# Gate and up projections of two feature blocks from seven half-width products in place of eight, in a two-layer fp32 decoder on one core

## Chip, cores and metric

The kernel runs on one core of a Trainium2 chip. The metric is the device time of one execution in microseconds (us). Before the change it was 2683.49 us, the median of 3 runs (2681.64 to 2683.74).

## What is computed

The reference is two layers of a decoder trunk on 512 tokens of width 1024. Each layer is a SwiGLU feed-forward block at half weight, a mixer (stick-breaking attention and a Mamba2 scan), and a second feed-forward block. The part that the change touches is the feed-forward block, of which there are four:

```
def swiglu(h, w_up, w_down):
    gate, up = jnp.split(h @ w_up, 2, axis=-1)
    return (jax.nn.silu(gate) * up) @ w_down
...
x = x + 0.5 * swiglu(rms_norm(x, ffn1_norm[l]), ffn1_w_up[l], ffn1_w_down[l])
```

The hidden width is 2816, that is 22 blocks of 128 features, each with a gate and an up column block of 1024 by 128 weights.

## The kernel before, in words

Activations lie with features on the 128 partitions and the 512 tokens along the free dimension, so `x` and the normed `h` are 8 tiles of 128x512. All products are made at fp32 accuracy from three products of a shorter format: a weight `w` and an activation are each split into a high part (`hi`, a cast) and the rest (`lo`, a subtraction), and `mm3` (lines 232 to 236) issues hi by hi, lo by hi and hi by lo into the same PSUM bank. Each is a matmul of 128x128 weights against 128x512 activations.

Weights come in units. A unit is what one output block needs: 8 blocks of 128x128 (128x1024, 512 KB) for gate or up, 8 or 6 for down. The order of all units is fixed by `unit_order`, and `unit` hands them out in that order. `fetch` loads a unit into one of three `wraw` buffers, `AHEAD` = 4 units early, over SyncE's queue. `convert` casts it on ScalarE into `whi` and subtracts on VectorE into `wlo`, `LOOK` = 2 units early, into one of three pairs of buffers, so the cast for unit p+2 needs the buffer that unit p-1 has just given back. `dense` runs a unit's 24 matmuls, and calls `tick` after each three: this lets the small generators in `self.side` (conversions, evictions, activations) each issue their next instructions. The order on TensorE, VectorE, ScalarE and GpSimd is the order in which this code issues; each engine works through its own list in order and waits at its head.

One feed-forward block (`ffn`) goes over three slices of 8, 8 and 6 feature blocks. For each feature block, `project` makes the gate product, then the up product, in one PSUM bank each; `gate` applies SiLU on ScalarE, `up` multiplies on VectorE and splits the result into `act`. After the blocks of a slice come 8 down products over that slice, each added to `x`. The first feature blocks of a block run on activations that are not yet scaled by the norm; `scale_blocks` makes scaled tiles `tt`, and during one up product (`swapped`) `h` is replaced by the split of these tiles.

PSUM has 8 banks: four for `mm`, two for `pa`, two for `pt`.

Of the kernel before, what the change touches and what calls it, by code (L numbers as in the profile page):

```python
# [7 lines left out]
F32 = mybir.dt.float32  # L8
F32R = mybir.dt.float32r
# [7 lines left out]
P = 128  # L17
# [13 lines left out]
FFN = 2816  # L31
FB = FFN // P
SLICES = ((0, 8), (8, 16), (16, 22))
EPS = 1e-6
KCONV = 4

# [46 lines left out]
            yield "dt", None  # L83


def unit_order(layer):

    def ffn(f):
        for s, (j0, j1) in enumerate(SLICES):
            for j in range(j0, j1):  # L90
                yield (layer, f, "gate", j), KB
                yield (layer, f, "up", j), KB
# [24 lines left out]


def all_units():
    table, off = {}, 0  # L120
    for layer in range(DEPTH):
        for key, n in unit_order(layer):
            table[key] = (off, n)
            off += n * P * P
    return table, off


class Builder:
# [8 lines left out]
    def __init__(self, ctx, tc, xT, wflat, par, taps, out):  # L137
        self.tc, self.nc = tc, tc.nc
        self.ctx = ctx
        self.xT, self.wflat, self.par, self.taps, self.out = xT, wflat, par, taps, out  # L140
        self.units, _ = all_units()
        self.keys = list(self.units)
        self.pos = 0
        self.raw, self.loaded = [], []
        self.count = 0
        self.side = []
        self.xd = None
        self.logs = True

    def name(self, s):  # L150
# [38 lines left out]
            self.room[tag] += 1  # L189


    def fetch(self, i):
        off, n = self.units[self.keys[i]]
        raw = self.t(self.wraw, [P, KB * P], "wraw")
        self.nc.sync.dma_start(raw[:, :n * P], self.wflat[off:off + n * P * P].rearrange("(p f) -> p f", p=P))
        self.raw.append(raw)

    def convert(self, i):

        nc = self.nc  # L200
        key = self.keys[i]
        n = self.units[key][1] * P
        raw, self.raw[i] = self.raw[i], None
        hi = self.t(self.wsp, [P, KB * P], "whi", F32R)
        lo = self.t(self.wsp, [P, KB * P], "wlo", F32R)
        nc.scalar.copy(hi[:, :n], raw[:, :n])  # L206
        yield 2
        nc.vector.tensor_tensor(lo[:, :n], raw[:, :n], hi[:, :n].bitcast(F32), op=ALU.subtract)  # L208
        self.loaded[i] = (hi, lo)

    def ahead(self):

        last = len(self.keys) - 1
        while len(self.loaded) <= min(self.pos + self.LOOK, last):
            i = len(self.loaded)
            while len(self.raw) <= i:
                self.fetch(len(self.raw))
            self.loaded.append(None)
            self.spawn(self.convert(i))
        while len(self.raw) <= min(self.pos + self.AHEAD, last) and len(self.raw) - len(self.loaded) < 2:  # L220
            self.fetch(len(self.raw))

    def unit(self, *key):
        assert self.keys[self.pos] == key, (self.keys[self.pos], key)
        self.ahead()
# [9 lines left out]
        mm(ps, a[1], b[0], start=False, stop=False, **kw)  # L235
        mm(ps, a[0], b[1], start=False, stop=stop, **kw)  # L236

    def dense(self, ps, w, rhs, k0, k1, start=True, stop=True, each=None):
        for k in range(k0, k1):
            ks = slice((k - k0) * P, (k - k0 + 1) * P)  # L240
# [10 lines left out]
    def project(self, *key, swap=False, aside=False):  # L251

        ps = self.t(self.pa, [P, SEQ], "pa") if aside else self.t(self.pmm, [P, SEQ], "mm")
        w, normed = self.unit(*key), self.normed
        if swap and not normed and self.scaled_blocks >= KB // 2:
            new = []
            each = self.swapped(new)
            for _ in range(len(self.hx)):  # L260
                next(each)
            self.dense(ps, w, self.h, 0, KB, each=each)
            self.h, self.normed = new, True
        else:
            self.dense(ps, w, self.h, 0, KB)
        return ps, normed
# [10 lines left out]
    def scale_blocks(self, gain):  # L277

        while self.rs is None:
            yield 1  # L280
        for k in range(KB):
            self.nc.vector.scalar_tensor_tensor(self.tt[k], self.x[k], gain[:, k:k + 1], self.rs,  # L282
                                                op0=ALU.mult, op1=ALU.mult)
            self.scaled_blocks = k + 1
            yield 1

    def open_norm(self, tiles, gain):
        self.tt, self.normed, self.scaled_blocks = tiles, False, 0
# [170 lines left out]
        self.gated[g.name] = True  # L459
        yield 1  # L460

    def up(self, pu, g, fp, ap, act):
        while not self.gated.pop(g.name, False):
            yield 1
        a = self.t(fp, [P, SEQ], "a")
        self.nc.vector.tensor_tensor(a, pu, g, op=ALU.mult)  # L466
        yield 1
        parts = self.pair(ap, ("act", "act"))
        yield from self.split(parts, a)
        act.append(parts)  # L470

    def down(self, pd, m, gain, last):
        x = self.x[m]
# [4 lines left out]
    def x_final(self, m, gain):  # L478
        x = self.x[m]
        yield 1  # L480
        if gain is not None:
            yield from self.norm_split(m, gain)
        else:
            self.xg.append(self.t(self.fin, [P, SEQ], "xg", bufs=KB))
        if m == 0:
            self.tables(True)
        yield from self.norm_square(m, gain is None)
# [6 lines left out]

    def ffn(self, layer, f, gain, gain_next):
        tc = self.tc
        with tc.tile_pool(name=f"act{layer}{f}", bufs=18, reuse_waits="tile") as ap, \
                tc.tile_pool(name=f"ffn{layer}{f}", bufs=3, reuse_waits="tile") as fp, \
                tc.tile_pool(name=f"hx{layer}{f}", bufs=self.SPARE, reuse_waits="tile") as hx, \
                tc.tile_pool(name=f"tt{layer}{f}", bufs=KB, reuse_waits="tile") as tp:  # L500
            self.hx = [self.pair(hx, ("xhi", "xlo")) for _ in range(self.SPARE)]
            self.gated = {}
            self.open_norm([self.t(tp, [P, SEQ], "tt") for _ in range(KB)], gain)
            for s, (j0, j1) in enumerate(SLICES):
                act = []
                last = s == len(SLICES) - 1
                for j in range(j0, j1):
                    g = self.t(fp, [P, SEQ], "g")
# [7 lines left out]
                    self.spawn(self.up(pu, g, fp, ap, act))  # L516
                for m in range(KB):
                    ps = self.t(self.pmm, [P, SEQ], "mm")
                    self.dense(ps, self.unit(layer, f, "down", s, m), act, 0, j1 - j0)
# [406 lines left out]
    def mixer(self, layer):  # L926
# [4 lines left out]
        self.hx = []  # L931
        first = []
        order = list(qkv_order())
        for i in range(4):
# [93 lines left out]
    def build(self):  # L1028
# [24 lines left out]
        for layer in range(DEPTH):  # L1053
# [5 lines left out]
        with tc.tile_pool(name="fin", bufs=KB, reuse_waits="tile") as self.fin:  # L1059
            self.xg = []  # L1060
            self.ffn(DEPTH - 1, 2, self.pars[DEPTH - 1][:, G_FFN2:G_FFN2 + KB], None)
            self.flush()
            for m in range(KB):
                nc.vector.tensor_tensor(self.xg[m], self.xg[m], self.rs, op=ALU.mult)
                nc.sync.dma_start(self.out[m], self.xg[m])
        self.xpool.__exit__(None, None, None)


# [6 lines left out]
def lay_out(inputs):  # L1075
# [6 lines left out]
    for layer in range(DEPTH):  # L1082
# [4 lines left out]
        grp = [w_in[:, group_cols(g)] for g in range(GROUPS)]  # L1087
        for key, n in unit_order(layer):
            kind = key[1] if key[1] not in (1, 2) else key[2]
            if kind in ("gate", "up"):  # L1090
# [77 lines left out]
```

## Time and profile before

| | |
|---|---|
| time, median of 3 runs | 2683.49 us |
| profiled execution's own time | 2681.88 us |
| its span, first to last instruction | 2680.2 us |
| mean granted TensorE clock | 0.997 |
| TensorE matmul busy | 2655.0 us (99%) |
| TensorE weight load busy | 2207.9 us (82%) |
| VectorE busy | 1362.3 us (51%) |
| ScalarE busy | 1092.5 us (41%) |
| GpSimd busy | 322.4 us (12%) |
| read from HBM | 261.43 MB |

In the profile, PE is TensorE's matmuls, PEld its weight loads (which run beside matmuls), DVE VectorE, ACT ScalarE, POOL GpSimd, SP SyncE. Matmuls overlap in their records: a row's duration is longer than the distance from its start to the next start, and it is the distance, here called the pitch, that says how many a stretch of time holds.

### The profile page before, as it was taken

Reading aid. Unit: us, or ns where it says so; the run is one execution under the profiler, and the core shown is the slowest. Engines: PE = TensorE matmul, PEld = TensorE weight load, DVE = VectorE, ACT = ScalarE, POOL = GpSimd, SP = SyncE. Lnnn points to the kernel's source line nnn. Section 1 sums busy time; section 2 is a strip of 40 time slices with the busy share of each in tenths; the row PEclk is TensorE's granted clock in tenths of the full one; section 3 lists DMA queues with packets and bytes.
Section 4 is the critical chain, followed back from the end, with each engine's and each line's share of the span. In section 5 each row is a group of like instructions: output and inputs, shape, how many; then the busy total and the mean of one; then the engine's idle time right before and its main releaser. Section 6 shows DMA issues by size and latency. Waiting matters only on the chain.

```text
span 2680.2 us, 31245 instructions
## 1 busy us (share of the span) xinstructions
PE 2655.0 (99%) x12264; PEld 2207.9 (82%) x12264; DVE 1362.3 (51%) x1946; ACT 1092.5 (41%) x1827; POOL 322.4 (12%) x472
## 2 busy tenths in 40 slices
PE   9999999999999999999999999999999999999998
PEld 7888888888888888888888888888888888888886
DVE  7333376565665473333553333766666745733333
ACT  5222246655554242222432223566555543422223
POOL 1000011133232010000100000112332310100001
PEclk9999999999999999999999999999999999999999
DMA  4322242233333423222232232423333243322322
GB/s 143 102 95 95 90 131 81 92 113 103 114 101 124 134 87 103 101 95 97 92 102 95 95 102 87 135 73 106 103 114 102 99 136 121 102 94 96 101 93 73
DMA packets 85828, 276.15 MB, mean 103 GB/s; under 512 B 10112, under 2 KB 10624, under 8 KB 85680
## 3 DMA queue, kind: packets, MB, share of 16 engines
q1 hardware_dynamic: 85392, 274.08, 31.3%
q8 instruction: 96, 1.57, 0.3%
q14 instruction: 52, 0.43, 0.1%
q10 hardware_dynamic: 288, 0.07, 0.0%
HBM read 261.43 MB, written 12.68 MB: 102 GB/s over the span
## 4 chain that ended last, share of the span: by engine, by line
PE 92%; DVE 5%; ACT 1%; issue 1%; DMA 0%; POOL 0%; DVEq 0%; ACTq 0%
PE mm L234 28%; PE mm L236 28%; PE mm L235 28%; PE pa L828 1%; PE pt L591 1%; DVE wlo L208 1%; PE pa L665 1%; DVE tt L282 1%; PE pa L830 1%; PE pt L813 1%; PE pt L811 1%; ACT whi L206 1%; DVE cv L729 0%; PE pa L235 0%; PE pa L236 0%
## 5 line engine op out<-in xcount | busy, mean ns | idle before, releaser
L234 PE MATMUL mm<-hhi,whi 128*128 128x512 f32 x2148 | 858.5, 400 | 0.0
L236 PE MATMUL mm<-hlo,whi 128*128 128x512 f32 x2148 | 838.9, 391 | 1.3 <-DVE hlo L274 1.3
L235 PE MATMUL mm<-hhi,wlo 128*128 128x512 f32 x2148 | 836.8, 390 | 0.0
L206 ACT CAST whi<-wraw 128x1024 fp32r<-128x1024 f32 (+2 forms) x472 | 473.9, 1004 | 870.8 <-PE mm L236 513.9
L208 DVE TENSOR_TENSOR wlo<-wraw,whi 128x1024 fp32r<-128x1024 f32 (+2 forms) x472 | 583.8, 1238 | 397.4 <-ACT whi L206 396.6
L236 PEld LDWEIGHTS mm<-hlo,whi 128*128 128x128 f32 x2148 | 403.3, 188 | 90.1 <-DVE hlo L274 3.4
L235 PEld LDWEIGHTS mm<-hhi,wlo 128*128 128x128 f32 x2148 | 404.3, 188 | 78.4 <-issue 1.2
L234 PEld LDWEIGHTS mm<-hhi,whi 128*128 128x128 f32 x2148 | 403.9, 188 | 77.4 <-issue 1.2
L236 PE MATMUL mm<-act,whi 128*128 128x512 f32 x704 | 273.9, 389 | 0.0
L234 PE MATMUL mm<-act,whi 128*128 128x512 f32 x704 | 273.9, 389 | 0.0
L235 PE MATMUL mm<-act,wlo 128*128 128x512 f32 x704 | 273.9, 389 | 0.0
L415 POOL TENSOR_TENSOR acc<-acc,sq 128x512 f32<-128x512 f32 x36 | 48.6, 1351 | 1525.3 <-ACT sq L408 1525.3
L474 DVE SCALAR_TENSOR_TENSOR x<-mm,x 128x512 f32<-128x512 f32 x96 | 66.1, 689 | 214.9 <-PE mm L236 214.9
L451 ACT ACTIVATE g<-mm 128x512 f32<-128x512 f32 x79 | 47.2, 598 | 292.7 <-PE mm L236 292.7
L466 DVE TENSOR_TENSOR a<-mm,g 128x512 f32<-128x512 f32 x87 | 60.1, 691 | 207.6 <-PE mm L236 202.9
L729 DVE SCALAR_TENSOR_TENSOR cv<-mm,conv,cv 128x511 f32<-128x511 f32 (+2 forms) x192 | 142.4, 742 | 24.7 <-ACT cv L726 22.9
L236 PEld LDWEIGHTS mm<-act,whi 128*128 128x128 f32 x704 | 132.1, 188 | 27.5
L234 PEld LDWEIGHTS mm<-act,whi 128*128 128x128 f32 x704 | 132.1, 188 | 27.5
L235 PEld LDWEIGHTS mm<-act,wlo 128*128 128x128 f32 x704 | 132.1, 188 | 27.3
L235 PE MATMUL mm<-xhi,wlo 128*128 128x512 f32 x316 | 122.9, 389 | 0.0
L234 PE MATMUL mm<-xhi,whi 128*128 128x512 f32 x316 | 122.9, 389 | 0.0
L236 PE MATMUL mm<-xlo,whi 128*128 128x512 f32 x316 | 122.9, 389 | 0.0
(233 smaller groups left out, 2923.0 us busy)
## 6 DMA issues: line engine op xcount, KB each, us to landing
wraw<-in_wflat_dram SPq DMA_DIRECT2D x392, 512.0 KB, 3.3
wraw<-in_wflat_dram SPq DMA_DIRECT2D x66, 384.0 KB, 3.1
cumb<-cum_d SPq DMA_DIRECT2D x16, 768.0 KB, 4.2
xd<-x SPq DMA_DIRECT2D x16, 256.0 KB, 4.0
wraw<-in_wflat_dram SPq DMA_DIRECT2D x16, 256.0 KB, 3.2
x<-xd SPq DMA_DIRECT2D x16, 256.0 KB, 4.9
gd<-gs SPq DMA_DIRECT2D x12, 256.0 KB, 2.0
gd<-gm SPq DMA_DIRECT2D x12, 256.0 KB, 2.0
```

The lines of the kernel that those rows point to most:

```text
L206: nc.scalar.copy(hi[:, :n], raw[:, :n])
L208: nc.vector.tensor_tensor(lo[:, :n], raw[:, :n], hi[:, :n].bitcast(F32), op=ALU.subtract)
L234: mm(ps, a[0], b[0], start=start, stop=False, **kw)
L235: mm(ps, a[1], b[0], start=False, stop=False, **kw)
L236: mm(ps, a[0], b[1], start=False, stop=stop, **kw)
L282: self.nc.vector.scalar_tensor_tensor(self.tt[k], self.x[k], gain[:, k:k + 1], self.rs, op0=ALU.mult, op1=ALU.mult)
L415: eng.tensor_tensor(self.acc, self.acc, sq, op=ALU.add)
L451: nc.scalar.activation(g, pg, AF.Silu)
L466: self.nc.vector.tensor_tensor(a, pu, g, op=ALU.mult)
L474: self.nc.vector.scalar_tensor_tensor(x, pd, 0.5, x, op0=ALU.mult, op1=ALU.add)
L591: self.nc.tensor.transpose(pt[:, cs], src[:, cs], self.ident)
L729: nc.vector.scalar_tensor_tensor(u[:, i:], ps[:, :SEQ - i], tap[KCONV - 1 - i], u[:, i:], op0=ALU.mult, op1=ALU.add)
```

## The change

A feed-forward block's gate and up products for two neighbouring feature blocks are seen as a 2 by 2 block product: on one side gate and up against the lower and upper half of the 1024 input features, on the other side the lower and upper half of the features against two halves of the tokens (columns 0 to 255 and 256 to 511). Winograd's form of Strassen's scheme makes the four results from seven products of half size in place of eight. It needs sums of weight blocks, sums of activation blocks, and sums of results.

- `unit_order` has a `pair` with seven units (`SEVEN`) in place of four. `pairs_from` begins the pairs at feature block 4, in the very first feed-forward block at 6; the earlier ones stay as they were. That is 9 pairs in three of the feed-forward blocks and 8 in the first, 35 in all.
- `pair_of_blocks` runs the seven products. Each unit has 24 matmuls as before, of 128x256 in place of 128x512 (8 weight blocks, four for each of the two feature blocks, three matmuls each): 168 matmuls of 128x256 in a pair, where there were 96 of 128x512. Two parts of the results pass through ScalarE copies and VectorE additions between products that go on in the same PSUM bank.
- Weights: `11`, `12` and `22` are loaded as before. The sums `s1` and `s3` are made by DMA: a plain load over SyncE's queue, then a second load over GpSimd's queue that adds to what is there. `s2` and `s4` are VectorE additions (`add`), spawned three units ahead, one before the unit's conversion.
- Activations: `combine` makes the sums on VectorE in halves of 256 columns once for each feed-forward block, after the swap, and splits them into `diff`.
- The first two down products of a slice are interleaved: both do all but their last two feature blocks, then both do these.
- Buffers: the split activations of two feature blocks share a tile, the final output takes its tiles from `hp`.

```diff
+SEVEN = ("11", "12", "s2", "s1", "s3", "s4", "22")
+STORED = ("11", "12", "s1", "22")
...
     def fetch(self, i):
+        key = self.keys[i]
+        raw = None
+        if "pair" not in key or key[-1] in ("11", "12", "22"):
+            raw = self.t(self.wraw, [P, KB * P], "wraw")
+            self.nc.sync.dma_start(raw[:, :self.units[key][1] * P], self.stored(key))
...
+        for key in self.early.get(i, ()):
+            base = key[:-1]
+            raw = self.sums[key] = self.t(self.sx, [P, KB * P], key[-1], bufs=2)
+            self.nc.sync.dma_start(raw, self.stored(base + ("s1",)))
+            self.nc.gpsimd.dma_start(raw, self.stored(base + ("22" if key[-1] == "s1" else "11",)), accum_op=ALU.add)
...
+    def combine(self):
+        nc, half = self.nc, SEQ // 2
+        a, b = slice(0, half), slice(half, SEQ)
+        for k in range(KB // 2):
+            u, v = self.tt[k], self.tt[k + KB // 2]
+            nc.vector.tensor_tensor(u[:, a], u[:, a], u[:, b], op=ALU.subtract)
+            nc.vector.tensor_tensor(u[:, b], v[:, b], u[:, b], op=ALU.subtract)
...
+            for i in (k, k + KB // 2):
+                yield 1
+                hi = self.th[i]
+                nc.scalar.copy(hi, self.tt[i])
+                yield 2
+                lo = self.t(self.tp, [P, SEQ], "tt", F32R)
+                nc.vector.tensor_tensor(lo, self.tt[i], hi.bitcast(F32), op=ALU.subtract)
...
+        def product(ps, part, rhs, cols, start):
+            hi, lo = self.unit(*base, part)
+            for j in range(2):
+                for k in range(n):
+                    ks = slice((j * n + k) * P, (j * n + k + 1) * P)
+                    self.mm3(ps[:, j * half:(j + 1) * half], (hi[:, ks], lo[:, ks]),
+                             [r[:, cols] for r in rhs[k]], start and j + k == 0, k == n - 1, skip_group_check=True)
+                    if k % 2:
+                        self.tick()
...
+        product(chain, "11", lower, a, True)
+        nc.scalar.copy(g1, chain)
+        product(ps2, "12", upper, a, True)
+        nc.vector.tensor_tensor(g1, g1, ps2, op=ALU.add)
+        self.spawn(activate(g1, up1, a))
+        product(chain, "s2", diff[n:], b, False)
+        nc.scalar.copy(g2, chain)
+        product(ps3, "s1", diff[:n], a, True)
+        c = self.t(fp, [P, SEQ], "c", bufs=2)
+        nc.scalar.copy(c, ps3)
+        product(chain, "s3", diff[:n], b, False)
+        nc.vector.tensor_tensor(c, chain, c, op=ALU.add)
+        up2.append(c)
+        product(ps3, "s4", upper, b, False)
+        nc.vector.tensor_tensor(g2, g2, ps3, op=ALU.add)
+        self.spawn(activate(g2, up2, b))
+        product(chain, "22", diff[n:], a, False)
+        up1.append(chain)
```

On TensorE, at the start of the first pair (feature blocks 6 and 7 of the first feed-forward block), there stand before the end of one up product and the start of the next gate product:

```order
L236 MATMUL mm_129_674<-hlo_96_487,whi_119_611 128x512
L234 MATMUL mm_134_707<-xhi_13_155,whi_125_645 128x512
L235 MATMUL mm_134_707<-xhi_13_155,wlo_126_646 128x512
L236 MATMUL mm_134_707<-xlo_14_156,whi_125_645 128x512
L234 MATMUL mm_134_707<-xhi_15_157,whi_125_645 128x512
```

and now, at the same place:

```order
L286 MATMUL mm_142_725<-hlo_104_498,whi_133_661 128x512
L284 MATMUL mm_148_759<-xhi_13_158,whi_140_698 128x256
L285 MATMUL mm_148_759<-xhi_13_158,wlo_141_699 128x256
L286 MATMUL mm_148_759<-xlo_14_159,whi_140_698 128x256
L284 MATMUL mm_148_759<-xhi_15_160,whi_140_698 128x256
```

The same triple of products stands there, with the same 128x128 weight load for each, but half the columns behind each load.

On VectorE, a steady stretch of two feature blocks has eight rows before (`wlo` is a weight subtraction, `a` the product of gate and up, `act` its low part):

```order
L208 TENSOR_TENSOR wlo_1148<-wraw_1076,whi_1147 128x1024
L466 TENSOR_TENSOR a_1179<-mm_1140,g_1107 128x512
L300 TENSOR_TENSOR act_1188<-a_1179,act_1187 128x512
L208 TENSOR_TENSOR wlo_1182<-wraw_1109,whi_1181 128x1024
L208 TENSOR_TENSOR wlo_1218<-wraw_1141,whi_1217 128x1024
L466 TENSOR_TENSOR a_1249<-mm_1210,g_1172 128x512
L300 TENSOR_TENSOR act_1258<-a_1249,act_1257 128x512
L208 TENSOR_TENSOR wlo_1252<-wraw_1174,whi_1251 128x1024
```

Of the sixteen rows that a pair has now, these nine stand from the addition after the sixth product (L594) to the next pair's fourth subtraction:

```order
L594 TENSOR_TENSOR g_244_1489<-g_244_1489,pa_242_1487 128x512
L236 TENSOR_TENSOR s2_266_1693<-s1_248_1523,wraw_254_1588 128x1024
L573 SCALAR_TENSOR_TENSOR a_267_1701<-c_258_1621,g_244_1489 128x512
L253 TENSOR_TENSOR wlo_265_1691<-wraw_259_1623,whi_264_1690 128x1024
L374 TENSOR_TENSOR act_239_1484<-a_267_1701,act_238_1483 128x2x256
L573 SCALAR_TENSOR_TENSOR a_275_1731<-mm_240_1485,g_243_1488 128x512
L374 TENSOR_TENSOR act_239_1484<-a_275_1731,act_238_1483 128x2x256
L253 TENSOR_TENSOR wlo_277_1734<-s2_266_1693,whi_276_1733 128x1024
L253 TENSOR_TENSOR wlo_280_1768<-s1_248_1523,whi_279_1767 128x1024
```

The next pair's addition for `s2` and its second subtraction now stand between the two halves of this pair's activation, and the subtraction for `s2` behind both.

More of the change, by code (lines that the diff above doesn't have):

```diff
@@ L90, in ffn @@
             for j in range(j0, j1):
-                yield (layer, f, "gate", j), KB
-                yield (layer, f, "up", j), KB
+                if j < pairs_from(layer, f):
+                    yield (layer, f, "gate", j), KB
+                    yield (layer, f, "up", j), KB
+                elif j % 2 == 0:
+                    for part in SEVEN:
+                        yield (layer, f, "pair", j, part), KB
             for m in range(KB):
@@ L123, in all_units @@
             table[key] = (off, n)
-            off += n * P * P
+            if "pair" not in key or key[-1] in STORED:
+                off += n * P * P
     return table, off
@@ L147, in __init__ @@
         self.xd = None
+        self.sums, self.early, self.summed = {}, {}, 0
+        for i, key in enumerate(self.keys):
+            if "pair" in key and key[-1] in ("s1", "s3"):
+                self.early.setdefault(i - (5 if key[-1] == "s1" else 4), []).append(key)
         self.logs = True
@@ L221, in ahead, with unit @@
             self.fetch(len(self.raw))
-    def unit(self, *key):
+        for i in range(self.summed, min(self.pos + self.LOOK + 1, last) + 1):
+            if self.keys[i][-1] in ("s2", "s4"):
+                self.spawn(self.add(self.keys[i]))
+            self.summed = i + 1
+    def unit(self, *key, ahead=True):
         assert self.keys[self.pos] == key, (self.keys[self.pos], key)
-        self.ahead()
+        if ahead:
+            self.ahead()
         w = self.loaded[self.pos]
@@ L263, in project @@
             self.h, self.normed = new, True
+            if self.th is not None:
+                self.spawn(self.combine())
         else:
@@ L460, in gate, with up @@
         yield 1
-    def up(self, pu, g, fp, ap, act):
+    def up(self, pu, g, fp, parts):
         while not self.gated.pop(g.name, False):
@@ L467, in up, with pair_of_blocks, activate @@
         yield 1
-        parts = self.pair(ap, ("act", "act"))
         yield from self.split(parts, a)
-        act.append(parts)
+    def pair_of_blocks(self, base, fp, two):
+        nc, half, n = self.nc, SEQ // 2, KB // 2
+        assert self.normed and self.combined == n
+        a, b = slice(0, half), slice(half, SEQ)
+        lower, upper = self.h[:n], self.h[n:]
+        diff = self.diff
+        chain, ps2 = (self.t(self.pmm, [P, SEQ], "mm") for _ in range(2))
+        ps3 = self.t(self.pa, [P, SEQ], "pa")
+        def product(ps, part, rhs, cols, start):
[7 more added lines that the diff above has]
+                        self.tick()
+        def activate(g, c, cols):
+            nc.scalar.activation(g, g, AF.Silu)
+            yield 1
+            while not c:
+                yield 1
+            r = self.t(fp, [P, SEQ], "a")
+            nc.vector.scalar_tensor_tensor(r, c[0], -1.0, g, op0=ALU.mult, op1=ALU.mult)
+            yield 1
+            r = r.rearrange("p (j t) -> p j t", j=2)
+            yield from self.split([t.rearrange("p (j t) -> p j t", j=2)[:, :, cols] for t in two], r)
+        up1, up2 = [], []
+        g1, g2 = (self.t(fp, [P, SEQ], "g", bufs=4) for _ in range(2))
+        product(chain, "11", lower, a, True)
[16 more added lines that the diff above has]
+        up1.append(chain)
@@ L507, in ffn @@
                 for j in range(j0, j1):
-                    g = self.t(fp, [P, SEQ], "g")
+                    if j % 2 == 0:
+                        two = self.pair(ap, ("act", "act"), (P, 2 * SEQ))
+                        act += [tuple(t[:, i * SEQ:(i + 1) * SEQ] for t in two) for i in range(2)]
+                    if j >= pairs_from(layer, f):
+                        if j % 2 == 0:
+                            self.pair_of_blocks((layer, f, "pair", j), fp, two)
+                        continue
+                    g = self.t(fp, [P, SEQ], "g", bufs=4)
                     if self.pos == 0:
@@ L1058, in build @@
                 self.ffn(layer, 2, par[:, G_FFN2:G_FFN2 + KB], self.pars[layer + 1][:, G_FFN1:G_FFN1 + KB])
[L1059 to L1065, printed above, removed]
+        self.xg = []
+        self.ffn(DEPTH - 1, 2, self.pars[DEPTH - 1][:, G_FFN2:G_FFN2 + KB], None)
+        self.flush()
+        for m in range(KB):
+            nc.vector.tensor_tensor(self.xg[m], self.xg[m], self.rs, op=ALU.mult)
+            nc.sync.dma_start(self.out[m], self.xg[m])
         self.xpool.__exit__(None, None, None)
@@ L1089, in lay_out @@
             kind = key[1] if key[1] not in (1, 2) else key[2]
-            if kind in ("gate", "up"):
+            if kind == "pair":
+                if key[-1] not in STORED:
+                    continue
+                r0, c0 = {"11": (0, 0), "12": (DM // 2, 0), "s1": (0, FFN), "22": (DM // 2, FFN)}[key[-1]]
+                c0 += key[3] * P
+                w = a[f"ffn{key[1]}_w_up"][layer][r0:r0 + DM // 2]
+                blk = np.concatenate([w[:, c0:c0 + P], w[:, c0 + P:c0 + 2 * P]])
+            elif kind in ("gate", "up"):
                 w = a[f"ffn{key[1]}_w_up"][layer]
```

63 lines of the change are left out of this document (50 added, 13 removed).

## The prediction

> **What bounds the kernel now.** I read the page first (busy shares), then what TensorE waits for, then TensorE's timeline in a feed-forward stretch, and last the few places where it already runs 256-column matmuls.
>
> ```profile
> span 2680.2 us, 31245 instructions
> PE 2655.0 (99%) x12264; PEld 2207.9 (82%) x12264; DVE 1362.3 (51%) x1946; ACT 1092.5 (41%) x1827; POOL 322.4 (12%) x472
> ```
>
> The waits of TensorE, longest in total first (us, times, longest):
>
> ```profile
> PE pt L423 <- DVE acc L415: 2.9, 3, 2.5
> PE pt L811 <- DVE yt L893: 2.0, 2, 1.0
> ```
>
> TensorE has matmuls in flight for 99% of the span, and its two longest waits in the whole run add up to 4.9 us. So there is nothing to win by removing waits; time goes only if the matmul stream itself gets shorter. The shape of that stream in a feed-forward block:
>
> ```profile
> 200.98 0.39 PE L234 MATMUL mm<-hhi,whi 128*128 128x512 f32 x1
> 201.21 0.39 PE L235 MATMUL mm<-hhi,wlo 128*128 128x512 f32 x1
> ...
> 204.83 0.39 PE L236 MATMUL mm<-hlo,whi 128*128 128x512 f32 x1
> 205.06 0.39 PE L234 MATMUL mm<-xhi,whi 128*128 128x512 f32 x1
> ```
>
> From 200.98 to 205.06 eighteen matmuls start: 4.08 / 18 = 0.2267 us each. That pitch, not the 0.39 us that a row shows as its duration, is the cost of one 128x512 matmul. The interleaving of the first two down products takes no wait away, since none is there: the two rows above are the largest, and neither is a down product.
>
> **The main term: 168 short matmuls for 96 long ones.** A pair of feature blocks has 96 x 0.2267 = 21.76 us of matmuls now. The change makes 168 of half the columns. If half the columns cost half the pitch (0.1133) it would be 19.04 us, a gain of an eighth. Break-even is 21.76 / 168 = 0.1295. So everything hangs on the pitch of a 128x256 matmul that loads its own weights. The trace has a few, in the attention:
>
> ```profile
> 404.76 0.28 PE L234 MATMUL pa<-yt,yt 128*128 128x256 f32 x1
> 404.88 0.28 PE L235 MATMUL pa<-yt,yt 128*128 128x256 f32 x1
> 405.00 0.28 PE L236 MATMUL pa<-yt,yt 128*128 128x256 f32 x1
> 405.12 0.40 PE L234 MATMUL mm<-hhi,whi 128*128 128x512 f32 x1
> ...
> 434.65 0.29 PE L234 MATMUL pt<-btok,yt 128*128 128x256 f32 x1
> 434.78 0.28 PE L235 MATMUL pt<-btok,yt 128*128 128x256 f32 x1
> 434.89 0.29 PE L236 MATMUL pt<-btok,yt 128*128 128x256 f32 x1
> 435.02 0.22 PE L234 MATMUL pt<-dec,yt 128*128 128x128 f32 x1
> ```
>
> Each is the same hi/lo triple as in the change. The first takes 0.36 / 3 = 0.120 a matmul, the second 0.37 / 3 = 0.123. I take 0.120, since the second stands between other short matmuls and the new products stand only among their like. The durations point the same way: 0.39 us at 512 columns less 0.28 at 256 is 0.11 for 256 columns, so a pitch of 0.2267 falls to about 0.117 and not to 0.1133. A matmul costs a little beyond its columns. 168 x 0.120 = 20.16 us, 1.60 us less than 21.76; for 35 pairs that is 56 us. With 0.123 it is 20.66, a gain of 1.10 and 38 us; with 0.1133 it is 2.72 and 95 us.
>
> The Trainium skill, page "TensorE: Matmul & The Clock Gate", section "Back-to-back issue gap", has a warm gap of columns / 2.4 ns plus 2.5 ns. That makes 215.8 ns for 512 columns and 109.2 for 256, an estimate of 20.72 - 18.34 = 2.38 us a pair or 83 us. The trace does not bear it out: its 226.7 ns at 512 columns is 10.9 ns above it.
>
> There is a floor below which no matmul with its own weights goes, since the load takes time too:
>
> ```profile
> 723.91 0.78 PE L828 MATMUL pa<-xdt,dec 128*128 128x64 f32 x6
> ```
>
> and the group that this row belongs to, with the mean duration of one:
>
> ```profile
> L828 PE MATMUL pa<-xdt,dec 128*128 128x64 f32 x384 | 49.8, 266 | 0.0
> ```
>
> Six matmuls of only 64 columns take 0.78 us; less the duration of the last, (0.78 - 0.266) / 5 = 0.103 a matmul. The load's floor is therefore just under what 256 columns cost, so the two should overlap, but with nearly nothing to spare.
>
> **What has to keep up.** A pair now takes VectorE and ScalarE more work in less time:
>
> ```profile
> L208 DVE TENSOR_TENSOR wlo<-wraw,whi 128x1024 fp32r<-128x1024 f32 x392 | 498.8, 1273 | 340.7 <-ACT whi L206 339.8 <-PE pt L591 0.6
> L300 DVE TENSOR_TENSOR act<-a,act 128x512 fp32r<-128x512 f32 x88 | 60.8, 692 | 76.4 <-ACT act L295 76.4
> L206 ACT CAST whi<-wraw 128x1024 fp32r<-128x1024 f32 x392 | 410.4, 1047 | 702.3 <-PE mm L236 403.1 <-issue 283.1 <-PE pa L236 14.2
> L295 ACT CAST act<-a 128x512 fp32r<-128x512 f32 x88 | 54.0, 614 | 27.5 <-DVE a L466 27.5
> ```
>
> VectorE: seven subtractions and two weight additions of 128x1024 (9 x 1.273 = 11.5 us), and seven operations of 128x512 (three additions of results, two products, two low parts, 7 x 0.69 = 4.8): 16.3 us in 20.16, 81%, where it had 4 x 1.273 + 4 x 0.69 = 7.9 in 21.76. ScalarE: seven casts (7.3) and seven 128x512 operations at about 0.61 (4.3): 11.6 us, 58%. Both fit. A unit now lasts 24 x 0.120 = 2.88 us and not 5.44, and a conversion has two units, 5.76 us, from the moment its buffer is free to its first use; cast and subtraction need 1.05 + 1.27 = 2.32 of these if nothing stands ahead.
>
> The tightest place is the stretch of VectorE's rows that the change shows. It starts when the sixth product ends. Up to the subtraction for `s2`, eight rows: 3 x 1.27 + 5 x 0.69 = 7.3 us, and two places where VectorE must wait for a ScalarE cast of 0.61. The next pair's third product starts three units later, at 8.64 us. So about half a microsecond is left: no wait if all goes to plan, a few tenths if not. What is queued behind this row is only the subtraction for `s1`, which has a whole unit more. I charge 0.1 us a pair, 3.5 us in all, with bounds of 0 and 0.5 (18 us).
>
> At the head of a feed-forward block, `combine` adds 16 operations on half tiles (at most 0.69 each) and 8 subtractions of 0.69 on VectorE, up to 16.6 us, between the swap and the first pair: two feature blocks, 4 x 5.44 = 21.8 us, in which VectorE has about 7.9 us of its own. That is 24.5 in 21.8, but the halves cost less than whole tiles and the sums are first read by the third product. I charge 1 us for each of four blocks, bounds 0 and 3.
>
> **Weights by DMA.** The sums `s1` and `s3` bring three more 512 KB transfers a pair, two of which add to what is in SBUF.
>
> ```profile
> q1 hardware_dynamic: 85392, 274.08, 31.3%
> ...
> wraw<-in_wflat_dram SPq DMA_DIRECT2D x392, 512.0 KB, 3.3
> L415 POOL TENSOR_TENSOR acc<-acc,sq 128x512 f32<-128x512 f32 x36 | 48.6, 1351 | 1525.3 <-ACT sq L408 1525.3
> ```
>
> 274 MB take 31.3% of 16 queues over 2680 us, so at full use 327 MB go through in a millisecond and 0.524 MB cost 1.6 us. Seven transfers are 11.2 us of a pair's 20.16, if an adding transfer costs what a plain one does. No row shows an adding transfer. The bounds: a plain one (3.3 us to landing) and three times as much. `fetch` issues the load for `s1` six units before the pair, and the addition for `s2` needs it five units later, 5 x 2.88 = 14.4 us: room for two plain landings and a third, 9.9 us. GpSimd's queue holds the adding transfers and, in order with them, only its additions at the end of a block (L415) and the first two gate products; so a wait there holds nobody in a slice up. On SyncE's queue the plain loads for `s1` and `s3` stand between those of the units; each costs its issue, and the unit behind has two units of time. I take nothing for all of this.
>
> At the very start two such pairs of loads stand in SyncE's order ahead of the loads of the second and third later units: 2 x 1.6 us, against a unit's 5.44. Nothing.
>
> **The sum.** 56 - 3.5 - 4 = 48 us. Made against the profiled execution's own 2681.88 us it gives 2634; the median of the runs lies 1.6 us above, so 2636.
>
> **Rivals.**
> 1. Half the columns, half the pitch. For it: the 0.120 was read beside other short work, not in a long run. Against: three in a row at 0.120, and the durations. 95 us less what is charged above: 2683.5 - 95 + 7.5 = 2596.
> 2. The feeding comes late (VectorE's row, or an adding transfer), and the wait goes to TensorE at the third or fifth product of each pair. For it: 81% on VectorE in strict order, and a kind of transfer without a row. At 0.5 us a pair it leaves 2683.5 - 56 + 18 + 4 = 2650, at 1 us 2667; it turns to a loss above 1.5 us a pair. If an adding transfer cost six plain ones, the queues alone would need (5 + 12) x 1.6 = 27 us a pair, 7 above the matmuls, and the time would be 2683.5 - 56 + 35 x 7 = 2873. It decides from 3.8 plain ones.
> 3. Slower: the weight load sets the pace on TensorE. Its place is the load behind each 256-column matmul. The rows where it happens:
>
> ```profile
> 411.37 0.33 PE L665 MATMUL pa<-xz,nones 128*128 128x128 f32 x2
> 411.55 0.45 PE L665 MATMUL pa<-xz,ntri 128*128 128x256 f32 x2
> 411.84 0.39 PE L234 MATMUL mm<-hhi,whi 128*128 128x512 f32 x1
> ```
>
> Two 256-column matmuls take 0.29 us, 0.145 each. If a long run behaves so, a pair is 24.4 us, 2.6 more than now: 2683.5 + 35 x 2.6 = 2775. It decides from 0.1295. Against it: here they follow 128-column ones, whose loads are already behind; in a run of 256 the floor of 0.103 leaves a little slack. But no run of more than three is in the trace. The same section of the Trainium skill's page says that the spacing in a sustained stream is set by matmul and load together, with 81 ns at 128 columns and 131 at 512: between these, by a straight line, 256 columns cost about 98, or 0.75 of the long one, where break-even is 0.57. That would be a loss too; the 0.227 of this trace for 512 columns is not that page's figure, so I give it no more chance than the rows do.
>
> **How the numbers follow.** Forecast (0.117 to 0.1235, feeding hidden; 2617 to 2655): 0.60. Rival 1: 0.10. Rival 2: 0.20, of which 0.11 still faster, 0.04 the same, 0.05 slower. Rival 3: 0.10, slower. That makes faster 0.81, same 0.04, slower 0.15, with 0.2% (5.4 us, about what a measurement of this kernel can tell from no change) as the bound. The range takes in the forecast's bounds, rival 1 with a few us to spare and rival 2 up to a little over 1 us a pair, and leaves out the slower cases and rival 2's worst: 2590 to 2672.
>
> **What would show it.** Right: 128x256 rows in a pair start 0.120 apart over a whole unit; a pair lasts about 20.2 us; TensorE's waits stay at a few us in all; VectorE is some 80% busy in pairs. A pitch over 0.1295 in a stretch without waits proves rival 3, a wait of TensorE's third or fifth product on VectorE or on the added loads rival 2, 0.113 rival 1. I would be wrong altogether if TensorE's granted clock fell in the pairs, which is 0.997 over the run now.

## The result and the profile after

The changed kernel takes 2643.51 us, the median of 4 runs (2640.51 to 2645.46). The kernel before, timed beside it, takes 2682.56 us (4 runs, 2680.95 to 2683.74). The ratio is 0.9854 [0.9837, 0.9871], or 39 us less. The forecast was 2636 us, 47 us less. So the direction and the main term came out, and 8 us are missing.

The profiled execution took 2640.51 us with a span of 2638.8 us, 41.4 us less than the 2680.2 of before. Its page:

```profile
span 2638.8 us, 37409 instructions
PE 2601.9 (99%) x14784; PEld 2283.0 (87%) x14784; DVE 1679.4 (64%) x2322; ACT 1276.1 (48%) x2069; POOL 383.6 (15%) x542
```

There are 2520 more matmuls, 35 pairs by 72, and TensorE is still busy for 99% of a shorter span. TensorE's timeline inside a pair (start, duration, the row):

```profile
209.75 0.28 PE L285 MATMUL mm<-th,wlo 128*128 128x256 f32 x1
...
212.51 0.28 PE L284 MATMUL pa<-th,whi 128*128 128x256 f32 x1
```

The second of these is the 23rd matmul behind the first: 2.76 / 23 = 0.120 us each, the pitch that was taken from three rows of the attention. It is so in all 35 pairs; one without waits lasts 20.15 to 20.16 us. All pairs together take 709.3 us, where the same blocks took 35 x 21.76 = 761.6 before: 52.3 us less, the waits at the heads of the blocks already included.

The waits of TensorE, longest in total first (us, times, longest):

```profile
PE mm L285 <- DVE wlo L253: 10.2, 9, 2.6
PE pt L497 <- DVE acc L489: 4.4, 4, 2.3
PE pt L959 <- DVE yt L1041: 2.0, 2, 1.0
```

The second row stood at 2.9 us before and has grown by 1.5; the third is what it was. The first row is new. Six of its nine waits are short and lie in the pairs at the heads of the feed-forward blocks. Three are 2.63 us each and lie elsewhere: in the down products of the last slice of the first three feed-forward blocks. TensorE there (in brackets the idle time ahead and what ended it):

```profile
340.32 0.39 PE L284 MATMUL mm<-act,whi 128*128 128x512 f32 x1
343.33 0.50 PE L285 MATMUL mm<-act,wlo 128*128 128x512 f32 x1 [2.63 <-DVE wlo L253]
```

Two starts 3.01 us apart, where 0.227 is the pitch: 2.78 us are lost each time, 8.4 in all. That is the place of the interleaved products, to which the prediction gave neither a price nor a rival.

52.3 - 8.4 - 1.5 = 42.4 us against the 41.4 measured by the spans. Of the last 1.0 us, 0.8 lies in the down products too: in the first three blocks the last slice takes 35.6 us where it took 32.64, which is 8.9 in all and not 8.4, and each of the other nine slices takes 0.03 more.

### The profile page after: what moved, and what is told of

It is laid out like the page before. It is cut to its first block, busy times and chain, and to the rows that moved or that the text cites. A ratio compares the mean times of both kernels' runs of the same rounds, so it can differ in the third digit from the quotient of the medians.

```text
span 2638.8 us, 37409 instructions
## 1 busy us (share of the span) xinstructions
PE 2601.9 (99%) x14784; PEld 2283.0 (87%) x14784; DVE 1679.4 (64%) x2322; ACT 1276.1 (48%) x2069; POOL 383.6 (15%) x542
## 3 DMA queue, kind: packets, MB, share of 16 engines
q1 hardware_dynamic: 90432, 292.43, 35.0%
## 4 chain that ended last, share of the span: by engine, by line
PE 86%; DVE 9%; ACT 2%; issue 1%; DMA 0%; POOL 0%; SPq 0%; DVEq 0%; ACTq 0%
PE mm L284 24%; PE mm L286 24%; PE mm L285 24%; PE pa L285 3%; PE pa L286 3%; PE pa L284 3%; DVE wlo L253 3%; PE pa L976 1%; PE pt L739 1%; PE pa L813 1%; DVE tt L334 1%; ACT whi L251 1%; PE pa L978 1%; PE pt L961 1%; DVE hlo L471 1%
## 5 line engine op out<-in xcount | busy, mean ns | idle before, releaser
L284 PE MATMUL mm<-hhi,whi 128*128 128x512 f32 (+1 forms) x1728 | 650.7, 377 | 0.0
L286 PE MATMUL mm<-hlo,whi 128*128 128x512 f32 (+1 forms) x1728 | 631.1, 365 | 1.2 <-DVE hlo L326 1.2
L285 PE MATMUL mm<-hhi,wlo 128*128 128x512 f32 (+1 forms) x1728 | 629.3, 364 | 0.6 <-DVE wlo L253 0.6
L285 PE MATMUL mm<-th,wlo 128*128 128x256 f32 x840 | 238.0, 283 | 1.7 <-DVE wlo L253 1.7
L286 PE MATMUL mm<-tt,whi 128*128 128x256 f32 x840 | 237.7, 283 | 0.0
L284 PE MATMUL mm<-th,whi 128*128 128x256 f32 x840 | 237.7, 283 | 0.0
L253 DVE TENSOR_TENSOR wlo<-s,whi 128x1024 fp32r<-128x1024 f32 x140 | 171.1, 1224 | 69.0 <-ACT whi L251 67.9
L601 DVE SCALAR_TENSOR_TENSOR x<-mm,x 128x512 f32<-128x512 f32 x96 | 66.1, 689 | 213.8 <-PE mm L286 213.8
L285 PEld LDWEIGHTS mm<-th,wlo 128*128 128x128 f32 x840 | 161.2, 192 | 2.3 <-DVE wlo L253 2.3
L284 PEld LDWEIGHTS mm<-th,whi 128*128 128x128 f32 x840 | 161.3, 192 | 0.0
L286 PEld LDWEIGHTS mm<-tt,whi 128*128 128x128 f32 x840 | 161.2, 192 | 0.0
```

Source lines behind the costliest of these rows:

```text
L284: mm(ps, a[0], b[0], start=start, stop=False, **kw)
L601: self.nc.vector.scalar_tensor_tensor(x, pd, 0.5, x, op0=ALU.mult, op1=ALU.add)
```

## The experiments

The theory after this reading: the seven products bring about 52 us, and the interleaving costs most of the difference to the 39. The rival: the interleaving is free or useful, and the missing time is lost in or around the pairs (VectorE's rows, the sums, the adding transfers). Unless the text says otherwise, a diff is against the changed kernel. Each time stands beside runs of the kernel before on the same chip.

**The interleaving taken out.**

```diff
-                n, both = j1 - j0, []
-                for m in range(2):
-                    both.append((self.t(self.pmm, [P, SEQ], "mm"), self.unit(layer, f, "down", s, m, ahead=m == 0)))
-                    self.dense(*both[m], act, 0, n - 2, stop=False)
+                n = j1 - j0
                 for m in range(KB):
-                    if m < 2:
-                        ps = both[m][0]
-                        self.dense(*both[m], act, n - 2, n, start=False, base=0)
-                    else:
+                    if True:
```

> The changed kernel with the down products of a slice one after the other, each unit handed out with its own look-ahead, as before the change. Theory (the interleave costs 2.6 us at the last slice of three feed-forward blocks, because the fourth down unit's cast is issued a unit late, behind the norm's work on ScalarE): TensorE's wait in a down product on the weight subtraction, 7.9 us in all, goes; at most 0.2 us comes back at the last two feature blocks of each first down product; 39 us faster than before becomes 47, near 2635.5 us. Rival (the interleave covers a wait for the last pair's activation, which stood before neither in the trace nor in the order): the first down product of each of 12 slices waits some 1 us, and the time is the changed kernel's or a few us more.

It took 2630.08 us (2629.73 to 2630.46), with 2681.81 for the kernel before: 0.9809 [0.9795, 0.9822], 51.7 us less than before and 13.4 less than the change. Its waits:

```profile
PE pt L497 <- DVE acc L489: 2.4, 1, 2.4
PE mm L285 <- DVE wlo L253: 2.2, 6, 0.6
```

The three long waits are gone, and only the six at the heads stay. The gain is larger than the waits that I had counted, because the waits on L497 at the end of a block go down too (4.4 to 2.4) and because of the clock (below).

Why the waits come can be read by setting the last slice of both kernels side by side. First VectorE in the kernel without the interleaving:

```profile
332.81 0.69 DVE L601 SCALAR_TENSOR_TENSOR x<-mm,x 128x512 f32<-128x512 f32 x1 [0.49 <-PE mm L286]
...
335.01 0.95 DVE L253 TENSOR_TENSOR wlo<-wraw,whi 128x768 fp32r<-128x768 f32 x1
```

The first down product ends just before 332.8, its result is added to `x` (L601), its buffer is free, and the subtraction for the fourth unit is under way at 335.0. In the changed kernel the two products share their end, so the first result comes later: its addition starts 7.0 us behind the slice's first matmul (at 328.05) where it was 4.3 (behind 328.48), and the second follows 2.15 us behind it; and no unit is asked for between them, so two casts come at once. ScalarE there:

```profile
335.81 0.72 ACT L469 ACTIVATE hhi<-x,par 128x512 fp32r<-128x512 f32 x1 [5.51 <-DVE x L601]
336.55 1.28 ACT L176 ACT_TABLE_LOAD   x1
337.84 0.63 ACT L479 ACTIVATE acc<-x 128x512 f32<-128x512 f32 x1
338.38 1.55 ACT L251 CAST whi<-wraw 128x768 fp32r<-128x768 f32 x2
339.84 0.72 ACT L469 ACTIVATE hhi<-x,par 128x512 fp32r<-128x512 f32 x1
```

And VectorE there:

```profile
335.08 0.69 DVE L601 SCALAR_TENSOR_TENSOR x<-mm,x 128x512 f32<-128x512 f32 x1 [3.19 <-PE mm L286]
...
340.59 0.75 DVE L471 SCALAR_TENSOR_TENSOR hlo<-x,par,hhi 128x512 fp32r<-128x512 f32 x1 [2.67 <-ACT hhi L469]
341.26 2.89 DVE L253 TENSOR_TENSOR wlo<-wraw,whi 128x768 fp32r<-128x768 f32 x2
```

The two casts stand behind the first steps of the next norm (L469, a table load, L479), the second result's `hhi` behind the casts, VectorE's `hlo` waits 2.67 us for that `hhi`, and behind `hlo` stands the subtraction that TensorE needs at 340.6. It starts at 341.26 and takes 2.02 us, since an addition of GpSimd runs beside it (last section). In the other slices no norm is queued there.

**The interleaving taken out in the last slice alone.**

```diff
-                for m in range(2):
+                for m in range(0 if last else 2):
...
-                    if m < 2:
+                    if m < len(both):
```

> The changed kernel with the interleave left out in the last slice of each feed-forward block alone. Theory: as the plain order everywhere, near 2635.5 us, since only last slices have the norm's work on ScalarE. If the interleave is worth something in the other eight slices, this is faster than the plain order by that; if it is not, the two agree within 1 us.

2629.9 us (2629.62 to 2631.2), 0.9809 [0.9795, 0.9822]: the same as without any interleaving. The whole price lies in the last slices, and in the other slices the interleaving brings nothing that shows.

**The interleaving alone, in the kernel before.** The diff is against the kernel before (`unit` and `dense` get the arguments that they have in the change, and the loop behind these lines is the change's).

```diff
...
+                n, both = j1 - j0, []
+                for m in range(2):
+                    both.append((self.t(self.pmm, [P, SEQ], "mm"), self.unit(layer, f, "down", s, m, ahead=m == 0)))
+                    self.dense(*both[m], act, 0, n - 2, stop=False)
...
```

> The kernel before with the interleave of the first two down products alone, no pairs. Theory: the same late cast in three last slices, 2.6 us each: 8 us slower than before (2690.5), all of it waits of TensorE's down products on the weight subtraction. Rival (the late cast comes from the pairs' load on ScalarE, VectorE and the queues, not from the interleave): within 1 us of before.

2694.57 us (2693.35 to 2695.58) against 2681.81: 1.0048 [1.0034, 1.0062], 12.8 us slower. The two parts add up: -51.7 + 12.8 = -38.9, and the change measured -39.05. That they agree so closely is partly luck, since the runs of the changed kernel alone lie 5 us apart. Its waits:

```profile
PE mm L236 <- DVE wlo L208: 7.9, 3, 2.6
PE pt L424 <- DVE acc L416: 3.2, 3, 2.3
```

The same three waits, without any pair in the program; so the rival, in which the pairs' work on VectorE makes them, is out. But 7.9 is less than 12.8. Windows of this run show what more is lost (the window, its length, busy time of PE, PEld, DVE, ACT and POOL, granted clock, and the share and GB/s of DMA):

```profile
1300.00:1318.00 18.00, 18.00 (x81) 14.92 (x80) 5.46 (x7) 4.03 (x6) 0.00 (x0) 1.00 0.24 76
1318.00:1330.00 12.00, 9.37 (x36) 7.32 (x35) 7.45 (x9) 7.20 (x10) 1.99 (x2) 0.86 0.20 60
1683.00:1695.00 12.00, 9.38 (x36) 7.31 (x35) 7.24 (x9) 7.21 (x10) 1.78 (x2) 0.86 0.30 97
```

The granted clock is 0.86 of full speed in the windows of two of the waits, and 1.00 ahead. 0.14 x 12 = 1.7 us of full clock are lost in each, which is 3.4 us at half speed. The third wait (the earliest, between 350 and 365 us) has no such stretch. Three waits at 2.78 and two of these make 11.8 us of 12.8. In the profiled execution, whose span is 13.7 us longer than that of before, the three slices account for 11.7, and 1.6 more lies ahead of the first of them, where its trace has two stretches at half clock and that of before one. The changed kernel's four runs were granted 0.997, 0.995, 0.997 and 0.995 on the mean, and the two at 0.995 are the two slowest, by 2 to 5 us.

**A cast between the two products.** If what matters is that no cast is asked for between the products, asking there should bring nearly all of the 13 us back.

```diff
                         self.dense(*both[m], act, n - 2, n, start=False, base=0)
+                        if m == 0:
+                            self.LOOK -= 1
+                            self.ahead()
+                            self.LOOK += 1
```

> The changed kernel with the interleave kept, but the fourth down unit's conversion issued right behind the first down product's last matmuls, ahead of the norm's work for that product. Theory (it is the place of this cast in ScalarE's order that costs, and with the wait go the half-clock stretches that follow it): no wait of a down product on a weight subtraction in the last slices, and the time of the plain down order, 2630 us within 2. Rival (the interleave itself costs, by the two products that end together): near the changed kernel's 2643 us.

2638.73 us (2638.38 to 2639.93), 0.9842 [0.9829, 0.9856]. The theory fell in the time: against the runs of the kernel before it gains 42.4 us where the change gains 39.05, so 3.4 of the 13 us came back. Its waits:

```profile
PE pt L497 <- DVE acc L489: 8.7, 4, 2.6
PE mm L285 <- DVE wlo L253: 2.1, 5, 0.6
```

The wait on `wlo` is gone, as wanted, and stands at the end of the block instead, at the norm's product L497, 8.7 us in all where it was 2.4. In the first three blocks this new wait is 2.03 or 2.04 us, and in this trace each time a stretch of 3.4 us at half clock follows, at most 1.7 us each; the three longer waits of the changed kernel's trace are followed by none. So a part of what did not come back is the clock (last section).

What is not cured is that the first result comes late. Counted from the slice's first matmul, the additions of the first, third and eighth result to `x` start at 7.0, 14.5 and 35.6 us, where they start at 4.3, 12.6 and 33.7 in the kernel without the interleaving: from the third on the lag stays at 1.9 us. VectorE can't make it up, because the last slice keeps it as busy as TensorE: for each down product an addition 0.68, a wait for ScalarE 0.79, `hlo` 0.75 and a subtraction 2.05 (their starts come 4.1 us apart), and a unit of TensorE is 18 x 0.2267 = 4.08 us. There is no slack in which a late start could be made good. The last slice of the fourth block bears this out: no `hhi` and `hlo` for a next norm stand there, its subtractions take 0.96 us at most, and the third result is on time, at 12.5 us in both kernels. So the order of the casts decides at which product the debt is paid.

**Fewer columns behind each load.** In each group of twelve matmuls of a pair, nine run on 192 columns and three on 256. The last 64 columns are left out of these nine, so the output is not the reference's.

```diff
-                    self.mm3(ps[:, j * half:(j + 1) * half], (hi[:, ks], lo[:, ks]),
-                             [r[:, cols] for r in rhs[k]], start and j + k == 0, k == n - 1, skip_group_check=True)
+                    w = 192 if k else half
+                    self.mm3(ps[:, j * half:j * half + w], (hi[:, ks], lo[:, ks]),
+                             [r[:, cols.start:cols.start + w] for r in rhs[k]], start and j + k == 0, k == n - 1, skip_group_check=True)
```

> The changed kernel, where three of four matmuls of each pair (all but the first feature block of a sum) run over 192 columns in place of 256: a quarter of these columns is left out, so that the output is not the reference's. Question: what makes 120 ns for 256 columns. If it is columns plus a fixed part (226.7 and 120.0 ns give 0.4167 ns a column and 13.3 ns), 192 columns start 93 ns apart. If the weight load has a floor just under 120 (112 ns from the second on in the runs of six 64-column matmuls), they start about 112 apart. If the weight load already sets the pace at 256, 120. A pair takes 24 x 7 x (0.25 x 0.120 + 0.75 x pitch): 16.8, 19.2 or 20.2 us.

One run: 2601.11 us. TensorE in a pair:

```profile
208.06 0.31 PE L284 MATMUL pa<-th,whi 128*128 128x256 f32 x1
...
208.76 0.27 PE L284 MATMUL pa<-th,whi 128*128 128x192 f32 x1
...
209.42 0.31 PE L284 MATMUL mm<-th,whi 128*128 128x256 f32 x1
```

Six matmuls of 192 columns start from 208.76 to 209.42: 0.110 us each; a whole pair takes 19.04 us, which makes 0.111. Were the pitch columns and a constant, drawn through 0.2267 at 512 and 0.120 at 256, it would be 0.093. So at 192 columns something else sets the pace at about 0.11. The kernel before has the same pace at 64 columns: within the groups of six on L828, which the prediction read, the first two starts lie 0.056 us apart and the others 0.111. A floor that does not depend on the columns fits the weight load; no run here tells the load from another fixed cost of a matmul. The 0.120 of the change lies 0.01 above it: so near was the floor, on which rival 3 rests, to setting the pace.

**No pair at the heads.** From here the diffs are against the kernel without the interleaving. The pairs of all four blocks begin at feature block 6.

```diff
-    return 6 if (layer, f) == (0, 1) else 4
+    return 6
```

> The plain down order, and pairs from feature block 6 in all four feed-forward blocks: three pairs fewer, two more feature blocks of time for the activation sums. Theory: TensorE's waits at the first pair of the last three feed-forward blocks (0.74 us each and a few tenths) go, and three pairs at 1.6 us are given back: 4.8 - 2.3 = 2.5 us slower than the plain down order, 2632.6. If the sums on VectorE cost more than these waits show, it is not slower.

2630.55 us (2629.96 to 2631.43), 0.9811 [0.9798, 0.9825]: the same, with three pairs less, and not the 2.5 us slower that were expected. The waits on `wlo` at the heads are gone from its list, and its 32 pairs take 20.15 each, 645.0 us. The three pairs given up took 709.3 - 645.0 = 64.3 us by the changed kernel's sum, and 3 x 21.76 = 65.3 as plain blocks: each brought 0.3 us rather than 1.6.

**The weight sums late.** The additions for `s2` and `s4` are made right ahead of their unit's cast, not a unit earlier.

```diff
+        if key[-1] in ("s2", "s4"):
+            yield from self.add(key)
...
-        for i in range(self.summed, min(self.pos + self.LOOK + 1, last) + 1):
-            if self.keys[i][-1] in ("s2", "s4"):
-                self.spawn(self.add(self.keys[i]))
-            self.summed = i + 1
```

> The plain down order, with the weight additions for s2 and s4 issued at the unit of their split, right ahead of the cast, and not a unit earlier. Theory (VectorE is 80% busy in pairs and the addition, the cast and the subtraction make 1.2 + 1.05 + 1.2 = 3.5 us of the two units' 5.76, if nothing stands ahead): a wait of at most a few tenths of a us a pair, 2630 to 2640 us. Rival (what stands ahead on VectorE, up to 4 us, comes on top): a wait of 1 us and more in each pair before the third or the sixth product, 2665 us or more.

2672.6 us (2669.02 to 2674.57), 0.9965 [0.9952, 0.9977]: 42.5 us or 1.2 us a pair slower than with the early sums. My expectation fell and the rival's time came. Its waits:

```profile
PE mm L282 <- ACT act L367: 10.6, 7, 2.1
PE mm L282 <- ACT g L579: 9.4, 13, 1.0
PE mm L283 <- DVE wlo L255: 6.1, 17, 0.4
```

The cast now has to wait for the addition ahead of it, and what stands behind that cast in ScalarE's queue (`g`, `act`) comes late as well. Only half of the loss lies where the rival put it: the 35 pairs take 730.2 us, 20.9 more, and the down products of the first two slices, which wait for `act`, 18.1 more. So without the sums a unit ahead, which the prediction only counted as VectorE time, four fifths of the gain are gone.

**No adding transfers.** `s1` and `s3` are then no sums, and the output is not the reference's.

```diff
-            self.nc.gpsimd.dma_start(raw, self.stored(base + ("22" if key[-1] == "s1" else "11",)), accum_op=ALU.add)
```

> The plain down order without the 70 transfers that add to what is in SBUF, so that s1 and s3 are not sums and the output is not the reference's. Theory: they are hidden wholly, so 2630 us within 1. Rival (they delay the plain loads behind them, or take VectorE's port): some us faster, most of it in pairs.

2630.66 us (2629.34 to 2630.88), 0.981 [0.9797, 0.9824], the same as with them. They are hidden entirely, as the prediction took them to be.

Of the kernels that compute the whole reference, the change without its interleaving, in the last slices (2629.9 us) or everywhere (2630.1), is the fastest, ahead of both the kernel before and the change; with three pairs less it is as fast (2630.55).

## Why the prediction was right, and where it was off

**The matmul stream: right.** 168 x 0.120 for 96 x 0.2267 was read from rows of before, and the pitch came out at 0.120 in every pair. 35 x 1.60 = 56 us of it stand in the change less what is lost at the heads. Rival 1 (0.113) is out. Rival 3 (the load) is out at 256 columns; at 192 a floor shows. The prediction read this floor as 0.103, because its mean took in the first of the five distances, 0.056; the other four are 0.111. So the load left 0.01 us of room and not 0.017. The choice of 0.120 over the 0.123 and 0.145 of other rows was an argument, and it held.

**The row of VectorE: charged 3.5 us, measured 0.** A steady pair has no wait on `wlo`. The window of 20 us in a pair:

```profile
207.50:227.50 20.00, 20.00 (x156) 19.39 (x155) 14.12 (x16) 10.44 (x14) 1.73 (x2) 1.00 0.75 197
```

VectorE is busy for 14.12 of 20 us, 71% where the prediction had 81%; ScalarE for 10.44, 52% for 58%. The prediction multiplied row durations, and these overlap by a tenth or so. Two 128x1024 subtractions in a row, of 1.22 us each:

```profile
1019.59 2.35 DVE L253 TENSOR_TENSOR wlo<-s,whi 128x1024 fp32r<-128x1024 f32 x2
```

The second starts 1.13 us behind the first, not 1.27. This order of work on VectorE is what the late sums overflow, so the cover was real but thin.

**The heads: charged 4 us, measured 3.9** (1.3 in each of the three later blocks, none in the first, whose pairs begin later). TensorE at the second block's first pair:

```profile
1013.81 0.28 PE L284 MATMUL mm<-xhi,whi 128*128 128x256 f32 x1
...
1020.87 0.39 PE L285 MATMUL mm<-th,wlo 128*128 128x256 f32 x1 [0.58 <-DVE wlo L253]
...
1055.40 0.40 PE L284 MATMUL mm<-act,whi 128*128 128x512 f32 x1
```

Two pairs take 41.59 us here, where twice 20.16 is 40.32. The reason was right: from 977 to 1024 us VectorE pauses only twice, for 0.69 and 0.51 us, in its work on the norm, `combine` and the splits. That the sum came out at 4 is in part luck, of three blocks over the charge and one without a loss.

**The adding transfers: charged 0, measured 0,** though one costs more than the lower bound. The queues and the issues (KB each, median us from issue to landing) on the page:

```profile
q1 hardware_dynamic: 90432, 292.43, 35.0%
q0 software_dynamic: 10080, 36.70, 8.0%
...
wraw<-in_wflat_dram SPq DMA_DIRECT2D x357, 512.0 KB, 3.7
...
s<-in_wflat_dram SPq DMA_DIRECT2D x70, 512.0 KB, 5.1
s<-in_wflat_dram POOLq DMA_DIRECT2D x70, 512.0 KB, 7.6
```

8.0% for 36.7 MB and 35.0% for 292.43: 0.218 and 0.120 for a MB, 1.8 plain ones, where rival 2's loss began at 3.8. 5.1 + 7.6 = 12.7 us to landing instead of 9.9, within the 14.4 that `fetch` leaves.

**The interleaving: the step that failed.** The prediction says that it "takes no wait away, since none is there", and goes on. That is right, and in all slices but the last of a block it brings nothing and costs nothing that shows. But a step that moves the work of ScalarE and VectorE by a unit was costed at nothing without naming what covers it. In the last slices of the first three blocks nothing does: it adds 12.8 us. The sum as it stands, 56 - 4 (heads) - 12.8, is 39.2 us, and 39.05 was measured, closer than the runs of either kernel agree among themselves. The prediction's 48 came so near only since 3.5 of it was charged to a row that cost nothing.

## What to carry to other kernels

Where the matmul stream itself is the bound, a change to it can be priced from rows of the same shape, wherever in the program they stand; here three rows gave the pitch. Look at each distance between starts, not at the mean alone, and say why one row is taken and another is not. What goes wrong is then in the small edits beside it: for each one that shifts when a result comes, look at the stretch in which the engines behind TensorE have no slack (here the last slice before a norm, 4.1 us of VectorE for 4.08 of TensorE), for there a delay is not made good. And undo each part by itself, since a change that wins on the whole can carry a part that loses.

## What the runs showed of the hardware

- A matmul with its own 128x128 weights starts 0.2267 us behind the one before at 512 columns and 0.120 at 256; a straight line through the two makes 13.3 ns and 0.4167 ns for each column, an estimate. At 192 columns the line gives 0.093 and 0.111 was measured, and at 64 columns it is 0.111 too: below that, fewer columns bring nothing. The Trainium skill, page "TensorE: Matmul & The Clock Gate", section "LDWEIGHTS (loading the stationary operand)", gives a load as its columns / 1.2 in ns, which for 128 columns makes an estimate of 107 ns; the 0.111 lies near that.
- A wait of TensorE can cost up to 1.7 us beyond its length, when 3.4 us at half clock follow it. In the kernel with the cast between the products this is so after a wait of 2.04 us:

```profile
367.49 1.61 PE L497 MATMUL pt<-acc,ones 128*128 128x512 f32 x2 [2.04 <-DVE acc L489]
```

```profile
358.00:372.00 14.00, 11.96 (x44) 8.90 (x43) 7.85 (x8) 5.01 (x7) 1.43 (x2) 0.88 0.55 175
```

  The Trainium skill, page "TensorE: Matmul & The Clock Gate", section "HAM oscillation — how this bites in real kernels", puts the rule at no idle gaps over about 3.4 us. Here a gap of 2.04 us was already enough, so the measurement speaks for a smaller bound.

  When it happens can be read from the clock records of the ten traces. Within each trace, all changes of the granted clock lie on one grid of 3.413 us, and a stretch at half clock is one slot of it: in the kernel above they begin at 368.00, 1323.73 and 1675.31 us, 280 and 103 slots apart. Of thirteen waits that put 1.95 us or more into a single slot, all were followed by a slot at half clock. Of those that put 1.86 us or less into any one slot, none was, but for one of 1.49 in the first 12 us of a run, which stays open; between the two, one wait of 1.88 was and a part of 1.93 was not. So a wait of 2.63 us in the changed kernel, which the grid cuts into 1.24 and 1.39, costs its length alone. In the kernel before with the interleaving the same wait costs 1.4 us more where 2.32 of it lie in one slot: that last slice takes 37.0 us, and the one whose wait was cut in two 35.6. Where the grid lies against the start of the program differs from run to run.
- A 128x768 subtraction on VectorE takes 0.95 us, and 2.05 when GpSimd's additions for the norm run beside it (the row at 335.01 in the part on the interleaving is one without). In the kernel without the interleaving twelve of these 64 subtractions run beside such an addition for 1.23 us and take 2.04 to 2.05 us; the others take 0.96 at most. One of the twelve, VectorE and then GpSimd:

```profile
339.09 2.04 DVE L253 TENSOR_TENSOR wlo<-wraw,whi 128x768 fp32r<-128x768 f32 x1
```

```profile
339.00 1.33 POOL L489 TENSOR_TENSOR acc<-acc,sq 128x512 f32<-128x512 f32 x1 [54.37 <-ACT sq L482]
```

  The Trainium skill, page "SBUF — State Buffer", section "Who interferes with whom", says that a VectorE instruction with two inputs from SBUF contends with a GpSimd instruction that reads SBUF; the trace agrees, with 1.1 us more beside an addition of 1.33. Without these 1.1 us VectorE would have about that much slack for each down product of the last slice, by an estimate from these rows; no run took the additions away.
